# Opening of a hybrid decoder layer: two of four modulation sums computed by TensorE in one PSUM row, decay weights prepared later

## The chip, the cores and the metric

The kernel runs on one core of a Trainium2 chip. The metric is device time in microseconds (us) of one execution, lower is better. The kernel before takes 2497.76 us (median of 3 runs, 2494.24 to 2498.12).

The core has five engines with their own instruction streams: TensorE (PE, matrix products; its loads of the stationary operand are counted apart as PEld), VectorE (DVE), ScalarE (ACT), GpSimd (POOL) and SyncE (SP), which here issues nearly all DMA transfers. Each engine runs its instructions in a fixed order; a wait of one instruction holds up all that stand behind it on that engine.

## The reference

One layer, one sequence of 2048 tokens, model width 1024, all in float32. What matters here is the modulation and the decay:

```python
c_act = jax.nn.silu(c)                                   # (1, 1024)
mod = (c_act @ w_ada[l] + b_ada[l])[:, None, :]          # (1, 1, 6144)
sh_m, sc_m, g_m, sh_f, sc_f, g_f = jnp.split(mod, 6, axis=-1)
h = rmsnorm(x, pre_mix_norm_w[l]) * (1.0 + sc_m) + sh_m
proj = h @ w_in                                          # 3592 columns, 8 of them decay and beta logits a, b
g = -jnp.exp(dn_a_log) * jax.nn.softplus(a + dn_dt_bias)
```

After the projection come a gated DeltaNet with four heads, a short gated convolution, the output projection and a squared-ReLU MLP (1024 to 4096 to 1024) with the same norm and modulation. `h` of the first block of tokens can't be had before `sc_m` and `sh_m` are known, which need the first 2048 columns of `w_ada` (8 MB).

## The kernel before, in words

Tokens are worked on in four blocks of 512. `hT` (tiles `h`) is the normed and modulated block, transposed: eight tiles, one for each 128 of the 1024 model columns. Exact products are made from split operands: each float32 weight and each `h` is cast to a high part by ACT (L250, L275) and the remainder is subtracted by DVE or POOL (L251, L274 to L276), and three matmuls (L336) add high-high, high-low and low-high.

**The opening** is the first block. `c_act` comes from `c` at L123. Shift and scale of the mixer are made in four quarters; quarter `qd` covers two of the eight `h` tiles. For each quarter `ada_load` (L150) brings eight pieces of `w_ada`, 128 x 512 each (256 columns of scale, 256 of shift): the first and third into four `sb` slots, the second and fourth into two `w1h` tiles. `ada_first` multiplies each piece by a column of `c_act` and sums the eight (L160 and L162, DVE) to `wt`, which still has to be summed over its 128 partitions. `ada_affine` does that with four narrow matmuls with a column of ones (L172), and four ACT operations (L177, L179) add bias and norm weight and leave the columns `mod_m`. Then come two projection weights for some quarters (`load_w1`: a transfer to `w1s`, L250, L251), the transposes of x (L265), the modulation and split of two `h` tiles (L272 or L274, L275, L276), and the projection of what there is so far (L336, into up to four PSUM accumulators). So work on `h` starts before the whole modulation is there.

**The decay weights** are the eight columns of `w_in` for the logits. Their split into `wab` (L382, L383) stands ahead of `pre_norm_first`. `neg_a` is made in `gating` (L487 to L490), which runs after the opening: 16 matmuls (L446, L448) and a DVE copy (L451) begin a chain of small DVE operations; the convolutions (L433 to L440) and the first transposes and products per head (L543 to L578) follow. L544 writes `bco`, which the products at L578 wait for.

**The gates** of the mixer and the MLP come from `ada_acc` (L129 to L133): eight pieces of 128 x 1024 per gate through three `w2h` buffers, multiplied and summed on DVE beside the opening's end and the first heads.

The order of instructions on each engine is laid out by a scheduler when the program is built. It works on the operations in program order and puts them where it expects their operands; `tc.issue_after(x)` holds back what is written in its block until `x`. The pools decide how many buffers of a name there are: `tp` and `pd` in PSUM two each, `acc` four, `w1h`, `w1s` and `w2h` three each. The head of the loop that calls the functions of the opening:

```python
for qd in range(4):
    acc = ada_first(quarters[qd])
    if 1 <= qd < 3:
        quarters.append(ada_load(qd + 1))
    mod[qd] = ada_affine(*acc, 84 + 2 * qd, 60 + 2 * qd, 76 + 2 * qd, f"m{qd}")
```

Of the kernel before, what the change touches and what calls it, by code (L numbers as in the profile page):

```python
# [13 lines left out]
ALU = mybir.AluOpType  # L14
# [18 lines left out]
def hybrid_layer(  # L33
# [40 lines left out]
    def ps_d():  # L74
        return psum.tile([P, 2, 256], F32, name="pd", bufs=2)
# [76 lines left out]
                                  .rearrange("(k p) f -> p k f", p=P))  # L152
        return sts

    def ada_first(sts):
        acc = small.tile([P, 2, 256], F32, name="wt", bufs=2).rearrange("p j i -> p (j i)")
        for k in range(KT):
            sj = sts[k // 2][:, (k % 2) * TB:(k % 2 + 1) * TB]
            if k == 0:
                V.tensor_scalar(out=acc, in0=sj, scalar1=c_act[:, 0:1], scalar2=None, op0=ALU.mult)  # L160
            else:
                V.scalar_tensor_tensor(out=acc, in0=sj, scalar=c_act[:, k:k + 1], in1=acc,  # L162
                                       op0=ALU.mult, op1=ALU.add)
        return [acc[:, 256:512], acc[:, 0:256]]

    def ada_affine(acc_sc, acc_sh, c_sc, c_w, c_sh, tag):

        ps = ps_tp()
        w = acc_sc.shape[-1] // P
        for n, acc in enumerate((acc_sc, acc_sh)):  # L170
            for j in range(w):
                T.matmul(out=ps[:, n * w + j:n * w + j + 1], lhsT=acc[:, j * P:(j + 1) * P],  # L172
                         rhs=ones[:, 0:1], start=True, stop=True)
        mod = const.tile([P, 2, w], F32, name="mod_" + tag)
        sc, sh = mod[:, 0], mod[:, 1]
        for j in range(w):
            A.activation(out=sc[:, j:j + 1], in_=ps[:, j:j + 1], func=AF.Identity,  # L177
                         scale=cols[:, c_w + j:c_w + j + 1], bias=cols[:, c_sc + j:c_sc + j + 1])
            A.activation(out=sh[:, j:j + 1], in_=ps[:, w + j:w + j + 1], func=AF.Identity,  # L179
                         bias=cols[:, c_sh + j:c_sh + j + 1])  # L180
        return sc, sh
# [197 lines left out]

    quarters.append(ada_load(1))  # L380
    wab = const.tile([P, KT, 16], F32R, name="wab")
    V.tensor_copy(out=wab[:, :, 0:8], in_=wab_s)  # L382
    V.tensor_tensor(out=wab[:, :, 8:16], in0=wab_s, in1=wab[:, :, 0:8], op=ALU.subtract)  # L383

    r0 = const.tile([P, 2, NT], F32, name="r0")
    for t in range(NT):
# [23 lines left out]
    def pre_norm_first(hT):  # L410

        mod, ws, pss = [None] * 4, [], []
        for qd in range(4):
            acc = ada_first(quarters[qd])
            if 1 <= qd < 3:
                quarters.append(ada_load(qd + 1))
            mod[qd] = ada_affine(*acc, 84 + 2 * qd, 60 + 2 * qd, 76 + 2 * qd, f"m{qd}")
            for f0 in EARLY[qd]:
                ws.append(load_w1(w_in, f0 * P, V, True, hold=False))
                pss.append(ps_acc())  # L420
            for half in range(2):
                to_hT(hT, xn0[2 * half:2 * half + 2], half, mod, range(2 * qd, 2 * qd + 2, 2),
                      A if qd < 3 else V)
            for i, w in enumerate(ws):
                new = i >= len(ws) - len(EARLY[qd])
                proj(pss[i], w, hT, ks=range(0 if new else 2 * qd, 2 * qd + 2))
# [15 lines left out]
    def gating(hT):  # L442
# [41 lines left out]
        V.tensor_scalar(out=xa, in0=xa, scalar1=0.0, scalar2=None, op0=ALU.max)  # L484
        g = small.tile(s3, F32, name="gg", bufs=1)
        V.scalar_tensor_tensor(out=g, in0=p, scalar=2.0, in1=xa, op0=ALU.mult, op1=ALU.add)
        if not ada.get("neg_a"):  # L487
            A.activation(out=neg_a, in_=alog, func=AF.Exp)
            V.tensor_scalar(out=neg_a, in0=neg_a, scalar1=-1.0, scalar2=None, op0=ALU.mult)
            ada["neg_a"] = True  # L490
        V.tensor_tensor(out=g, in0=g, in1=bc(neg_a[:, None, :], s3), op=ALU.mult)
        gh = small.tile([P, 2, NT, NH], F32R, name="ghl", bufs=1)
        V.tensor_copy(out=gh[:, 0], in_=g)
# [671 lines left out]
```

## Time and profile before

| what | value |
|---|---|
| median of 3 runs | 2497.76 us |
| the profiled execution | 2501.52 us |
| its span in the trace | 2499.8 us |
| PE busy | 2416.5 us, 97% |
| PEld busy | 2011.4 us, 80% |
| DVE busy | 1764.7 us, 71% |
| ACT busy | 1170.9 us, 47% |
| POOL busy | 237.0 us, 9% |

The shares are averages over the span. Rows below give times from the span's start. "PEclk" is the clock of TensorE that was granted, 1.00 being 2.4 GHz and 0.50 being 1.2 GHz. A row in brackets ends with the idle time of the engine just before it and what ended that. Where several instructions of a line follow each other, a row holds them all, with their count behind the x. The time of one is better read from the distance of starts, since matmuls overlap.

### The profile page before, as it was taken

The page shows a single profiled execution, that of the slowest core. Times are in us where ns is not written, and L with a number is a line of the kernel's source. Part 1 is how long each engine was busy: PE and PEld are TensorE (multiplying, and loading weights), DVE is VectorE, ACT ScalarE, POOL GpSimd, SP SyncE. Part 2 cuts the span into 40 slices and gives each one's busy share as a digit, 9 for nine tenths or more (in the row PEclk, how much of TensorE's full clock was granted, in tenths as well). Part 3 has the DMA queues.
Part 4 walks back from the last instruction along what each step waited for, and adds up shares of the span by engine and source line. Part 5 has one row for each costly group of instructions (what it writes and reads, how often), then busy time and mean ns, then how long its engine had stood idle before and what let it go on. Part 6 is the DMA issues. An engine that isn't in the chain of part 4 may idle for free.

```text
span 2499.8 us, 33806 instructions
## 1 busy us (share of the span) xinstructions
PE 2416.5 (97%) x11874; PEld 2011.4 (80%) x11874; DVE 1764.7 (71%) x3833; ACT 1170.9 (47%) x2402; POOL 237.0 (9%) x391
## 2 busy tenths in 40 slices
PE   5889999999999999999999999999999999999998
PEld 3678887788778888888878888888887888888887
DVE  6777795877885568576697657756679556857675
ACT  5533552444563245544466145544456424654432
POOL 2513010000040201000012020000002120100000
PEclk9999999999999999999999999999999999999999
DMA  7788489855664542544475544345557454344453
GB/s 246 266 292 267 168 292 310 283 177 169 202 234 156 172 153 103 156 147 127 136 245 193 184 154 143 102 135 152 160 164 249 143 169 168 110 144 135 125 161 101
DMA packets 297268, 449.53 MB, mean 180 GB/s; under 512 B 39189, under 2 KB 195978, under 8 KB 282250
## 3 DMA queue, kind: packets, MB, share of 16 engines
q1 hardware_dynamic: 295584, 447.27, 54.5%
q8 instruction: 94, 1.54, 0.3%
q14 instruction: 76, 0.62, 0.1%
q10 hardware_dynamic: 1514, 0.09, 0.0%
HBM read 376.01 MB, written 71.30 MB: 179 GB/s over the span
## 4 chain that ended last, share of the span: by engine, by line
PE 75%; DVE 13%; DMA 7%; ACT 3%; issue 2%; POOL 0%; SPq 0%; ACTq 0%; DVEq 0%
PE acc L336 41%; PE acc L341 24%; DVE t L438 2%; DMA w2h<-in_w_ff_dram 2%; DMA w2h<-in_w_ada_dram 1%; PE pd L704 1%; DMA w1s<-in_w_ff_dram 1%; PE pd L336 1%; DMA ws<-w2h 1%; DVE w1h L251 1%; DVE sb L935 1%; PE pd L560 1%; PE tp L265 1%; PE tp L692 1%; DVE sb L850 1%
## 5 line engine op out<-in xcount | busy, mean ns | idle before, releaser
L336 PE MATMUL acc<-h,w1h 128*128 128x512 f32 x5184 | 1219.6, 392 | 0.0
L336 PEld LDWEIGHTS acc<-h,w1h 128*128 128x128 f32 x5184 | 968.2, 188 | 196.0 <-ACT w1h L250 0.2
L341 PE MATMUL acc<-w1h,sa 128*128 128x512 f32 x2556 | 594.6, 392 | 7.9 <-ACT w1h L250 4.1
L341 PEld LDWEIGHTS acc<-w1h,sa 128*128 128x128 f32 x2556 | 478.3, 188 | 110.0 <-DVE w1h L251 7.0
L251 DVE TENSOR_TENSOR w1h<-w1s,w1h 128x1024 fp32r<-128x1024 f32 x333 | 406.5, 1221 | 152.8 <-ACT w1h L250 152.6
L250 ACT CAST w1h<-w1s 128x1024 fp32r<-128x1024 f32 (+1 forms) x343 | 359.6, 1048 | 289.2 <-PE acc L341 195.9
L959 DVE TENSOR_TENSOR t<-t 128x512 f32<-128x512 f32 (+1 forms) x148 | 91.3, 620 | 182.0 <-ACT t L958 179.2
L958 ACT ACTIVATE t<-acc 128x512 f32<-128x512 f32 (+1 forms) x132 | 73.7, 558 | 246.7 <-PE acc L336 246.3
L276 POOL TENSOR_TENSOR h<-t,h 128x256 fp32r<-128x256 f32 x70 | 59.6, 857 | 1251.9 <-ACT h L275 1246.6
L438 DVE SCALAR_TENSOR_TENSOR t<-cb,cols,t 128x512 f32<-128x512 f32 x144 | 119.1, 831 | 65.7 <-ACT t L436 63.9
L251 DVE TENSOR_TENSOR w2h<-sa,w2h 128x512 fp32r<-128x512 f32 x128 | 87.5, 687 | 35.7 <-ACT w2h L250 35.1
L336 PE MATMUL acc<-h,sa 128*128 128x256 f32 (+1 forms) x672 | 102.6, 308 | 4.0 <-POOL h L276 1.5
L250 ACT CAST w2h<-sa 128x512 fp32r<-128x512 f32 x128 | 78.5, 619 | 58.7 <-DVE w2h L251 33.2
L341 PE MATMUL acc<-w2h,sa 128*128 128x512 f32 x420 | 101.4, 393 | 0.0
L336 PEld LDWEIGHTS acc<-h,sa 128*128 128x128 f32 x672 | 90.2, 195 | 10.5 <-POOL h L276 3.8
L925 DVE TENSOR_TENSOR sb<-acc,sb 128x512 f32<-128x512 f32 x148 | 96.4, 681 | 2.0 <-PE acc L341 2.0
L341 PE MATMUL acc<-w2h,sb 128*128 128x512 f32 x384 | 95.2, 400 | 1.8 <-DVE sb L842 0.9
L341 PEld LDWEIGHTS acc<-w2h,sa 128*128 128x128 f32 x420 | 77.7, 188 | 15.5
L341 PEld LDWEIGHTS acc<-w2h,sb 128*128 128x128 f32 x384 | 72.3, 191 | 20.6 <-DVE sb L842 2.8
L250 ACT CAST sa<-t 128x256 fp32r<-128x256 f32 (+1 forms) x145 | 70.5, 487 | 27.2 <-DVE t L959 26.9
L251 DVE TENSOR_TENSOR sa<-t,sa 128x256 fp32r<-128x256 f32 (+2 forms) x145 | 75.3, 520 | 4.0 <-ACT sa L250 1.4
L234 ACT ACTIVATE jk_w<-sb 128x512 bf16<-128x512 f32 x64 | 40.3, 630 | 58.9 <-DVE sb L876 31.1
(285 smaller groups left out, 2748.4 us busy)
## 6 DMA issues: line engine op xcount, KB each, us to landing
w1s<-in_w_ff_dram SPq DMA_DIRECT2D x213, 512.0 KB, 3.9
w1h<-wc SPq DMA_DIRECT2D x86, 1024.0 KB, 4.9
w1s<-ws SPq DMA_DIRECT2D x112, 512.0 KB, 4.0
wc<-w1h SPq DMA_DIRECT2D x30, 1024.0 KB, 7.3
sa<-in_x_dram SPq DMA_DIRECT2D x32, 512.0 KB, 4.8
w1s<-in_w_in_dram SPq DMA_DIRECT2D x32, 512.0 KB, 5.4
w2h<-in_w_ada_dram SPq DMA_DIRECT2D x32, 512.0 KB, 5.3
sa<-in_w_out_dram SPq DMA_DIRECT2D x32, 512.0 KB, 3.8
```

Source lines behind the costliest of these rows:

```text
L234: A.activation(out=junk(DM, "w")[:, :src.shape[-1]], in_=src, func=AF.Square, scale=float(DM) ** -0.5, accum_out=s)
L250: A.copy(out=hi, in_=src)
L251: eng.tensor_tensor(out=lo, in0=src, in1=hi, op=ALU.subtract)
L265: T.transpose(out=tp[:, j * 256 + i * P:j * 256 + (i + 1) * P], in_=xn[i][:, (k0 + j) * P:(k0 + j + 1) * P], identity=ident)
L276: (G if j or eng is A else V).tensor_tensor(out=hT[k][:, 1, cs], in0=tmp, in1=hT[k][:, 0, cs], op=ALU.subtract)
L336: T.matmul(out=ps[:, c0:c1], lhsT=w[a][:, k, :], rhs=hT[k][:, b, c0:c1], start=(k == 0 and n == 0), stop=(k == KT - 1 and n == 2))
L341: T.matmul(out=ps, lhsT=lhs[a], rhs=rhs[b], start=(start and n == 0), stop=(stop and n == 2))
L438: V.scalar_tensor_tensor(out=tmp, in0=cb[:, w:w + TB], scalar=conv_w[:, w, ft:ft + 1], in1=tmp, op0=ALU.mult, op1=ALU.add)
L560: T.matmul(out=pk[:, t - tp0], lhsT=kq[h][:, 0, t * P:(t + 1) * P], rhs=kq[h][:, :, t * P:(t + 1) * P], start=True, stop=True)
L925: V.tensor_tensor(out=accs[key], in0=ps, in1=accs[key], op=ALU.add)
L958: A.activation(out=a[:, c0:c1], in_=ps[:, c0:c1], func=AF.Relu)
L959: V.tensor_tensor(out=a[:, c0:c1], in0=a[:, c0:c1], in1=a[:, c0:c1], op=ALU.mult)
```

## The change

`ada_first` gets a flag `on_pe`, set for quarters 1 and 3 (the second and the fourth). With it the sum over the eight pieces and over the 128 partitions is one accumulation of eight float32 matmuls: the stationary operand is a column of `c_act` (128 x 1), the moving one is the piece (128 x 512), and the result is one row of 512 in a `pd` buffer. ACT copies the row to the first partition of `wt`. `ada_affine` then turns the row into columns with matmuls whose contraction is one long (`ones[0:1, 0:1]`). Quarters 0 and 2 stay on DVE. `decay_weights` now holds the split of `wab` and the two operations on `neg_a`, and is written behind the third quarter's last DVE sum.

```diff
+    def ada_first(sts, on_pe):
         acc = small.tile([P, 2, 256], F32, name="wt", bufs=2).rearrange("p j i -> p (j i)")
+        if on_pe:
+            ps = ps_d().rearrange("p a b -> p (a b)")[0:1, :]
+            acc = acc[0:1, :]
         for k in range(KT):
             sj = sts[k // 2][:, (k % 2) * TB:(k % 2 + 1) * TB]
-            if k == 0:
+            if on_pe:
+                T.matmul(out=ps, lhsT=c_act[:, k:k + 1], rhs=sj, start=(k == 0), stop=(k == KT - 1))
+            elif k == 0:
                 V.tensor_scalar(out=acc, in0=sj, scalar1=c_act[:, 0:1], scalar2=None, op0=ALU.mult)
             else:
-                V.scalar_tensor_tensor(out=acc, in0=sj, scalar=c_act[:, k:k + 1], in1=acc,
-                                       op0=ALU.mult, op1=ALU.add)
+                ada["sum"] = V.scalar_tensor_tensor(out=acc, in0=sj, scalar=c_act[:, k:k + 1], in1=acc,
+                                                    op0=ALU.mult, op1=ALU.add)
+        if on_pe:
+            A.copy(out=acc, in_=ps)
...
-                         rhs=ones[:, 0:1], start=True, stop=True)
+                         rhs=ones[0:acc.shape[0], 0:1], start=True, stop=True)
...
-    V.tensor_copy(out=wab[:, :, 0:8], in_=wab_s)
-    V.tensor_tensor(out=wab[:, :, 8:16], in0=wab_s, in1=wab[:, :, 0:8], op=ALU.subtract)
+    def decay_weights():
+        V.tensor_copy(out=wab[:, :, 0:8], in_=wab_s)
+        V.tensor_tensor(out=wab[:, :, 8:16], in0=wab_s, in1=wab[:, :, 0:8], op=ALU.subtract)
+        A.activation(out=neg_a, in_=alog, func=AF.Exp)
+        V.tensor_scalar(out=neg_a, in0=neg_a, scalar1=-1.0, scalar2=None, op0=ALU.mult)
...
-            acc = ada_first(quarters[qd])
+            acc = ada_first(quarters[qd], qd % 2)
+            if qd == 2:
+                with tc.issue_after(ada["sum"].ins):
+                    decay_weights()
...
-        if not ada.get("neg_a"):
-            A.activation(out=neg_a, in_=alog, func=AF.Exp)
-            V.tensor_scalar(out=neg_a, in0=neg_a, scalar1=-1.0, scalar2=None, op0=ALU.mult)
-            ada["neg_a"] = True
```

The diff moves line numbers. In the changed kernel L165 is the new matmul, L172 the new ACT copy and L167/L169 the DVE sums (before L160/L162); L181 is before's L172, L274 its L265, L345 its L336, L283/L285 its L274/L276, L260 its L251, L393/L394 its L382/L383, L396 its L489, L462/L464 its L446/L448, L467, L473 and L475 its L451, L457 and L459, L454 its L438, L560 its L544.

On PE, around the second quarter's sum, the order before (`ones,wt` are the sums over partitions, `ident,sa` the transposes of x, `acc` the projection; numbers behind `h` tell tiles apart):

```order
L172 MATMUL tp<-ones,wt 128x1 x4
L265 MATMUL tp<-ident,sa 128x128 x8
L172 MATMUL tp<-ones,wt 128x1 x4
L265 MATMUL tp<-ident,sa 128x128 x3
L336 MATMUL acc<-h_201,sa 128x512
L265 MATMUL tp<-ident,sa 128x128
L336 MATMUL acc<-h_201,sa 128x512 x2
L336 MATMUL acc<-h_202,sa 128x512 x3
L265 MATMUL tp<-ident,sa 128x128 x4
```

and of the changed kernel:

```order
L181 MATMUL tp<-ones,wt 128x1 x4
L165 MATMUL pd<-w1h,c_act 1x512
L274 MATMUL tp<-ident,sa 128x128 x4
L165 MATMUL pd<-w1h,c_act 1x512 x3
L274 MATMUL tp<-ident,sa 128x128 x4
L165 MATMUL pd<-w1h,c_act 1x512 x3
L345 MATMUL acc<-h_199,sa 128x512 x3
L345 MATMUL acc<-h_200,sa 128x512 x3
L165 MATMUL pd<-w1h,c_act 1x512
L181 MATMUL tp<-ones,wt 128x1 x4
L274 MATMUL tp<-ident,sa 128x128 x8
```

The second quarter's eight matmuls lie between the transposes of the first, and the first six projection matmuls stand ahead of the last of them.

On PE, at the fourth quarter, the order before (between its sum over partitions and `gating` 60 L336 follow, of which the first are here):

```order
L336 MATMUL acc<-h_206,sa 128x512 x3
L172 MATMUL tp<-ones,wt 128x1 x4
L265 MATMUL tp<-ident,sa 128x128 x4
L336 MATMUL acc<-h_201,sa 128x512 x2
L265 MATMUL tp<-ident,sa 128x128 x4
```

and of the changed kernel (four more L165 of this quarter stand further up, between transposes and projection of the third; L462 and L464 are `gating`):

```order
L345 MATMUL acc<-h_203,sa 128x512 x3
L345 MATMUL acc<-h_204,sa 128x512 x3
L165 MATMUL pd<-w1h,c_act 1x512 x3
L181 MATMUL tp<-ones,wt 128x1 x4
L274 MATMUL tp<-ident,sa 128x128 x8
L462 MATMUL tp<-h_199,wab 16x512
L464 MATMUL tp<-h_199,wab 8x512
```

All of the projection work on the first six `h` tiles now lies ahead of the fourth quarter's sum, and only the last 24 projection matmuls (tiles 205 and 206, after the fifth L462) behind it.

On DVE, around the copy that begins `gating`, the order before:

```order
L251 TENSOR_TENSOR w1h<-w1s,w1h 128x1024
L276 TENSOR_TENSOR h_207<-t_503,h_207 128x256
L131 TENSOR_SCALAR gate_m<-w2h,c_act 128x1024
L451 COPY t_552<-tp 16x512
L457 COPY t_559<-tp 128x64
L459 TENSOR_TENSOR ab<-t_559 128x32
```

and of the changed kernel:

```order
L131 TENSOR_SCALAR gate_m<-w2h,c_act 128x1024
L283 TENSOR_SCALAR t_496<-tp,mod_m_486 128x256
L133 SCALAR_TENSOR_TENSOR gate_m<-w2h,c_act,gate_m 128x1024
L285 TENSOR_TENSOR h_205<-t_496,h_205 128x256
L283 TENSOR_SCALAR t_509<-tp,mod_m_486 128x256
L133 SCALAR_TENSOR_TENSOR gate_m<-w2h,c_act,gate_m 128x1024
L285 TENSOR_TENSOR h_205<-t_509,h_205 128x256
L133 SCALAR_TENSOR_TENSOR gate_m<-w2h,c_act,gate_m 128x1024 x2
L467 COPY t_558<-tp 16x512
L133 SCALAR_TENSOR_TENSOR gate_m<-w2h,c_act,gate_m 128x1024
L473 COPY t_565<-tp 128x64
L133 SCALAR_TENSOR_TENSOR gate_m<-w2h,c_act,gate_m 128x1024
```

Before, one operation of the mixer's gate stands ahead of that copy; now five do, and two more stand between it and the next steps of `gating`. On SP the loads of the gates' pieces follow suit: 13 of them stand ahead of the eleventh weight load to `w1s`, where 7 did. From some 290 us on the order is the same in both.

## Rows read from the trace of the kernel before

**Rows 1.** Stretches: us, busy time by engine, PE clock, DMA share, GB/s.

```profile
33.00:43.00 10.00, 8.12 (x23) 5.62 (x23) 9.75 (x10) 5.94 (x16) 5.88 (x6) 1.00 0.89 293
53.00:72.00 19.00, 18.95 (x89) 13.65 (x88) 5.72 (x7) 9.47 (x18) 8.05 (x6) 1.00 0.81 257
72.00:133.00 61.00, 47.03 (x220) 37.92 (x221) 55.21 (x97) 35.22 (x76) 33.05 (x26) 0.96 0.70 243
133.00:290.00 157.00, 155.09 (x861) 132.26 (x860) 121.86 (x286) 66.55 (x176) 28.28 (x53) 0.99 0.81 273
```

**Rows 2.** PE in order of time: start us, us, what [idle before, releaser].

```profile
23.03 1.87 PE L172 MATMUL tp<-ones,wt 128*128 128x1 f32 x8 [14.84 <-DVE wt L162]
39.61 3.31 PE L336 MATMUL acc<-h,sa 128*128 128x512 f32 x6 [1.46 <-ACT h L275]
44.86 0.65 PE L265 MATMUL tp<-ident,sa 128*128 128x128 f32 x4
49.65 0.96 PE L336 MATMUL acc<-h,sa 128*128 128x512 f32 x3 [1.33 <-POOL h L276]
...
132.43 1.09 PE L578 MATMUL tp<-ident,sa 128*128 128x128 f32 x4 [9.22 <-DVE bco L544]
```

**Rows 3.** The chain that ended last, 55 to 114 us: start us, us, what.

```profile
55.11 13.19 PE acc L336 x58
...
96.46 7.04 POOL w1h L251
...
105.04 8.12 DMA w2h<-in_w_ada_dram
```

**Rows 4.** DVE in order of time, opening.

```profile
14.40 0.20 DVE L382 CAST wab<-t 128x64 fp32r<-128x64 f32 x1 [12.05 <-DMA t<-in_w_in_dram]
...
23.69 5.47 DVE L162 SCALAR_TENSOR_TENSOR wt<-w1h,c_act,wt 128x512 f32<-128x512 f32 x7
...
34.19 7.86 DVE L162 SCALAR_TENSOR_TENSOR wt<-sb,c_act,wt 128x512 f32<-128x512 f32 x7
```

**Rows 5.** SP in order of time, and a DMA issue row (count, size, us to landing).

```profile
14.40 0.88 SPq L150 DMA_DIRECT2D sb<-in_w_ada_dram  x2
...
sb<-in_w_ada_dram SPq DMA_DIRECT2D x16, 256.0 KB, 6.4
```

**Rows 6.** One float32 product with 512 columns elsewhere in the kernel.

```profile
603.00 1.88 PE L192 MATMUL tp<-gate_f,ones 128*128 128x512 f32 x4
```

**Rows 7.** Line 446, matmuls of 16 stationary columns: least/median/most ns, first and last start.

```profile
L446 PE MATMUL tp<-h,wab x32: 388/396/402, 68.1 to 1891.8; 128*16 128x512 f32 x32
```

**Rows 8.** ACT in order of time.

```profile
39.76 1.05 ACT L250 CAST sa<-w1s 128x1024 fp32r<-128x1024 f32 x1
...
44.54 0.27 ACT L179 ACTIVATE mod_m<-tp,cols 128x1 f32<-128x1 f32 x1
...
99.95 0.58 ACT L433 COPY cb<-acc 128x512 f32<-128x512 f32 x1
```

**Rows 9.** DVE in order of time, from the start of gating to 133 us.

```profile
72.02 0.68 DVE L451 COPY t<-tp 16x512 f32<-16x512 f32 x1 [11.47 <-PE tp L448]
...
74.06 0.74 DVE L438 SCALAR_TENSOR_TENSOR t<-cb,cols,t 128x512 f32<-128x512 f32 x1
...
78.05 1.27 DVE L133 SCALAR_TENSOR_TENSOR gate_m<-w2h,c_act,gate_m 128x1024 f32<-128x1024 f32 x1
...
87.41 3.45 DVE L133 SCALAR_TENSOR_TENSOR gate_m<-w2h,c_act,gate_m 128x1024 f32<-128x1024 f32 x1
...
101.71 4.16 DVE L438 SCALAR_TENSOR_TENSOR t<-cb,cols,t 128x512 f32<-128x512 f32 x2 [0.45 <-ACT t L436]
...
113.19 1.28 DVE L133 SCALAR_TENSOR_TENSOR gate_m<-w2h,c_act,gate_m 128x1024 f32<-128x1024 f32 x1 [4.49 <-DMA w2h<-in_w_ada_dram]
...
118.08 2.91 DVE L438 SCALAR_TENSOR_TENSOR t<-cb,cols,t 128x512 f32<-128x512 f32 x1
...
127.60 2.86 DVE L438 SCALAR_TENSOR_TENSOR t<-cb,cols,t 128x512 f32<-128x512 f32 x1
```

More of the change, by code (lines that the diff above doesn't have):

```diff
@@ L153, in ada_load @@
         return sts
-    def ada_first(sts):
+    def ada_first(sts, on_pe):
         acc = small.tile([P, 2, 256], F32, name="wt", bufs=2).rearrange("p j i -> p (j i)")
+        if on_pe:
+            ps = ps_d().rearrange("p a b -> p (a b)")[0:1, :]
+            acc = acc[0:1, :]
         for k in range(KT):
             sj = sts[k // 2][:, (k % 2) * TB:(k % 2 + 1) * TB]
-            if k == 0:
+            if on_pe:
+                T.matmul(out=ps, lhsT=c_act[:, k:k + 1], rhs=sj, start=(k == 0), stop=(k == KT - 1))
+            elif k == 0:
                 V.tensor_scalar(out=acc, in0=sj, scalar1=c_act[:, 0:1], scalar2=None, op0=ALU.mult)
             else:
-                V.scalar_tensor_tensor(out=acc, in0=sj, scalar=c_act[:, k:k + 1], in1=acc,
-                                       op0=ALU.mult, op1=ALU.add)
+                ada["sum"] = V.scalar_tensor_tensor(out=acc, in0=sj, scalar=c_act[:, k:k + 1], in1=acc,
+                                                    op0=ALU.mult, op1=ALU.add)
+        if on_pe:
+            A.copy(out=acc, in_=ps)
         return [acc[:, 256:512], acc[:, 0:256]]
```

## The prediction, made before the changed kernel ran

> **What bounds the kernel now.** I read the busy shares first, then the opening by stretches, then PE's own order of time with the waits in it, then the chain that ended last, and last DVE and ACT where PE waits. PE is 97% busy over the whole span, so what matters is where it is not. From 133 to 290 us it works 155.09 of 157 [rows 1], and from about 290 us on both kernels have one order; a shift at 133 us is therefore carried to the end unchanged. What happens before has four stages.
>
> Up to 23 us PE waits: its first sum over partitions starts at 23.03 after 14.84 of idleness, released by DVE's first quarter [rows 2]. From 33 to 43 it is busy 8.12 of 10, and DVE, which sums the quarters, 9.75 [rows 1]. From there PE is bound by itself: the reader is to see one wait of 1.33, at 49.65, and between 53 and 72 it works 18.95 of 19 [rows 1, 2]. The chain names its work there: 58 projection matmuls in 13.19 [rows 3]. The third stage ends with the copy that begins gating, at 72.02, for which DVE had waited 11.47 [rows 9]. In the fourth, DVE is the bound: 55.21 of the 61 us to 133, and PE's wait of 9.22 before 132.43 is ended by DVE's `bco` [rows 1, 2]. So the question is what the change does to two dates: the copy at 72.02, and the release at 132.43.
>
> **What the change removes and adds.** DVE loses two sums of eight operations. PE gets 16 float32 matmuls of 512 columns; ACT two copies. The trace has no such matmul with one stationary column. Its nearest rows: the float32 products at 603.00 take 1.88 for two of them (each stands in the trace as two records), so 0.94 each [rows 6], against 13.19/58 = 0.23 for a projection matmul of as many columns [rows 3]. Fewer stationary columns don't help: of the matmuls of gating, with 16 and 8 columns, 16 stand between the first start, 68.1 [rows 7], and the copy at 72.02 [rows 9], 0.24 each, no less than a projection matmul. I take 0.94, with 0.23 as the lower end and 1.9 as the upper: PE ran at half rate in the early opening. Six projection matmuls at 39.61 take 3.31 [rows 2], and they would take 1.4 at 0.23; from 43 us on the distance of starts is 0.23.
>
> **Stage 1, to the first quarter's sum.** The decay weights' cast holds DVE until 14.40, waiting 12.05 for a transfer [rows 4]. With it moved behind the third quarter `c_act` can come some 4 us sooner. But two of the first quarter's pieces are issued only at 14.40 to 15.28 and land 6.4 later by the median [rows 5], near 21 to 22; the last two products have to follow. Before, the first quarter's sum ended at about 23.0. I take 1 us of gain (0 to 1.3).
>
> **Stage 2, second quarter.** Before, DVE's seven products behind the first take 5.47 from 23.69 [rows 4]. After, the eight matmuls stand between transposes, and PE has gaps there (10 - 8.12 = 1.9 in 33 to 43 [rows 1], more before). At 0.94 they are 7.5, at half rate 15. The sum would be in PSUM at 36 to 38, or at 43; then the copy (0.58 [rows 8]), eight small matmuls and four ACT operations make the second quarter's modulation ready near 40 (39 to 46), later than DVE made it. What follows is late by as much: the second weight's cast (39.76 [rows 8]) goes to about 42, and since its subtraction stands in DVE's order ahead of the last two products of the third quarter, the third sum ends near 45, where it ended at 42.05 (34.19 + 7.86 [rows 4]). The third modulation, ready at 44.8 before [rows 8], comes near 49.5. So far this costs little. At 49.65 before had 70 of its 96 projection matmuls still to do (the 58 of the chain's row, the three at 49.65 and nine between them); the changed order has 72 behind the third modulation.
>
> By the Trainium skill, "TensorE: Matmul & The Clock Gate", section "What's actually happening", the throttled clock is the default and activity releases it. That speaks for the change, which gives PE work where it had waited. If the full rate came at 30 rather than 43 us, some 12 projection matmuls would each save 0.2 and nine transposes 0.1, 3.5 in all, and the sum below would be lower by that. The windows before carry a granted clock of 1.00 throughout the opening [rows 1], while six matmuls took 3.31 [rows 2]: they don't show the level there, so I keep this out of the sum.
>
> **Stage 3, to the copy that begins gating.** The working for before: at 49.65, 70 projection matmuls of 0.23 (16.2), eight transposes of 0.16 (0.65/4 [rows 2]; 1.3), eight records of sums over partitions (half of the 1.87 at half rate [rows 2], 0.95), 16 gating matmuls (3.7) make 22.15, so 71.8 against the 72.02 seen. After, from the same 49.65: 72 x 0.23 = 16.6, seven of the fourth quarter's float32 matmuls at 0.94 = 6.6, 16 transposes 2.6, 0.95 and 3.7: 30.4, 8.3 more. The last quarter's chain adds the copy (0.58) and ACT's and DVE's modulation and split behind it, with only nine gating matmuls (2 us) as cover; before, 60 projection matmuls covered all of this. I add 1. The copy comes 9.5 later (5 if the fp32 matmuls fall into waits of PE or the clock comes sooner; 14 if the last quarter's chain lies open).
>
> **Stage 4, to the release of `bco`.** DVE goes on from the copy. By the order, 10 gate products and 30 convolution products stand before between the copy and the first L555 behind it; after, 11 and 27, so one more of 1.27 and three fewer of 0.74 [rows 9]: -0.95. DVE's wait of 4.49 at 113.19 was for a piece of the gate whose transfer took 8.12 behind a POOL split of 7.04 [rows 3, 9]. Its issue now stands ahead of the weight loads; it may go: 0 to -4.5. But 13 gate loads, where there were seven, stand ahead of the eleventh weight load on SP, and all of them share three buffers that DVE must free. Behind such a load a weight waits, behind the weight a head's projection, and behind that the convolution products: new waits of 0 to 4. Two gate products also stand between the steps of gating, 1.27 each. I take -4.5 for the wait, +2 for the new ones and -0.95: -3.5 (-5.4 to +3). PE's own clock and the seven projection matmuls that changed sides of the stall cancel to under 1.6, which I leave out.
>
> The sum: 9.5 - 3.5 = +6. DVE's 16 removed operations count for nothing here: their time was DVE's in stage 2, which PE's sum replaces by a later one. On the profiled execution that is 2501.52 + 6 = 2507.5. The median of the runs is 3.8 below that execution, so the time is 2497.76 + 6 = 2503.8. This case's own range is 2500 to 2509.
>
> **Rivals.**
>
> *The late gating is swallowed.* The chain from 96 to 113 goes through POOL's split, SP and the gate's transfer, not through gating [rows 3]. If these keep their dates, DVE's order after 113 does too, and a copy 9.5 late is made good out of the 9.22 that PE waits at 132.43 anyway. Against it: DVE is busy 55.21 of 61 there, without slack for a start 9.5 later. Time 2498 to 2500, taken as 2499.
>
> *The fourth stage shortens by more than the opening grows.* Four DVE operations in it are far above their usual length: 3.45 for 1.27, 4.16 for two of 0.74, 2.91 and 2.86 for 0.74 [rows 9], 9.2 in excess. If they find their places elsewhere, and the wait of 4.49 goes with no new one, the stretch from copy to release shrinks from 60.4 by 0.95 + 4.5 + 9.2 = 14.6 to 45.8, against 9.5 lost: -5.1, 2492.7. It decides when the stretch takes under 50.9. For it: POOL was busy 33.05 in those 61 us [rows 1], so the long ones depend on where POOL's work falls. Against it: the amount of POOL work is the same.
> The Trainium skill, "SBUF — State Buffer", section "SBUF: two separate sides", says that a DVE operation with two SBUF inputs and a POOL operation lock each other out of a shared port pair. The rows agree: the seven products took 7.86 beside POOL's work and 5.47 where it had little [rows 4]. By that rule the excess would move rather than go.
>
> *PE stays at half rate.* If the second quarter's eight matmuls run at 1.9 each and the modulation is ready only at 46, the third comes some 5 later: +11, 2509. For it: the earlier stretch of PE did not leave half rate until 43. Against it: the new matmuls fill gaps.
>
> That the change does not do what it says I rule out; the order shows it.
>
> **Chances.** The forecast 0.50, the swallowed start 0.25, the shorter fourth stage 0.15, half rate 0.10. A measurement of this kernel can tell about 0.2%, 5.0 us, from no change: 2492.8 and 2502.8 are the bounds. Of the forecast's own range some four fifths lie above 2502.8 (0.39), and all of half rate (0.10): slower 0.49. Of the shorter stage most lies beyond 2492.8 (0.13): faster 0.13. The rest is same: 0.38. For 8 in 10 the range goes from 2493, where the shorter stage begins to be left out, to 2512, three above half rate for a chain of the last quarter that lies open.
>
> **What would show it.** In the profile after: starts of the new matmuls (L165) 0.94 apart (0.23 would take 11 us of the cost away); the third modulation at 49.5 and the fourth near 71 (49.65 + 48 x 0.23 + 6.6 + 1.3 + copy, sums and ACT 2); the gating copy (L467) at 81.5; PE busy near full from 50 to there; DVE's wait for a gate piece gone or replaced by a wait behind weights; the stall before the products per head (L590) ending at 138.4. The forecast is wrong if the copy comes before 77, or if from copy to release takes less than 51 or as much as 60.

## The result and the profile after

The changed kernel takes 2520.32 us (median of 4 runs, 2519.33 to 2523.12), the kernel before 2497.94 in the runs beside it: ratio 1.0087, 95% interval 1.0075 to 1.01. That is 22.4 us slower, where 6 had been predicted and 14 was the far end of the range. The direction was right and the loss in the opening lay where it was predicted; some 9 us more arose behind the release of `bco`, in a stretch that had been taken as fixed.

The profiled execution after took 2523.12 us, with a span of 2521.4 against 2499.8. PE is busy 2439.8 us where it was 2416.5, DVE 1760.5 where it was 1764.7: the 16 operations taken from DVE barely show, while the 16 products given to PE hold it for 17.6 of the 23.3 us more. The stretches that answer to [rows 1] (us, busy time and count of PE, PEld, DVE, ACT, POOL, then PE clock, DMA share, GB/s), with the two stretches of half clock that matter below:

```profile
33.00:43.00 10.00, 7.14 (x29) 2.95 (x27) 5.90 (x7) 5.45 (x14) 3.28 (x5) 0.90 0.87 287
53.00:72.00 19.00, 17.00 (x72) 10.81 (x71) 5.44 (x5) 6.82 (x15) 7.93 (x5) 0.99 0.81 276
72.00:143.00 71.00, 58.60 (x255) 45.18 (x253) 62.30 (x103) 38.70 (x84) 30.42 (x29) 0.91 0.73 247
143.00:300.00 157.00, 153.05 (x839) 129.39 (x838) 118.04 (x278) 63.20 (x160) 31.46 (x54) 0.99 0.76 253
140.10:146.90 6.80, 4.80 (x17) 4.09 (x17) 4.43 (x17) 4.14 (x15) 0.52 (x2) 0.50 0.74 252
300.50:310.70 10.20, 8.88 (x29) 7.72 (x30) 2.54 (x5) 4.19 (x17) 0.00 (x0) 0.50 0.00 0
```

The fourth row is the one to compare with the last of [rows 1]. Before, the 157 us behind the release of `bco` held 2 us of idle PE; after, as many hold 4, and right behind them the granted clock falls to half for 10.2 us. Before, the corresponding fall lasts 3.4 us:

```profile
288.90:292.30 3.40, 3.40 (x10) 2.63 (x9) 0.69 (x1) 2.31 (x10) 0.00 (x0) 0.50 0.00 0
```

PE's own order of time after (start us, us, what [idle before, releaser]), the rows that answer to [rows 2]:

```profile
20.66 1.87 PE L181 MATMUL tp<-ones,wt 128*128 128x1 f32 x8 [12.53 <-DVE wt L169]
22.45 1.87 PE L165 MATMUL pd<-w1h,c_act 128*1 128x512 f32 x2
...
29.88 2.73 PE L165 MATMUL pd<-w1h,c_act 128*1 128x512 f32 x6
...
40.41 0.73 PE L345 MATMUL acc<-h,sa 128*128 128x512 f32 x2 [1.80 <-ACT sa L259]
...
47.37 0.95 PE L181 MATMUL tp<-ones,wt 128*128 128x1 f32 x8
...
64.99 2.74 PE L165 MATMUL pd<-w1h,c_act 128*1 128x512 f32 x6
68.39 1.05 PE L181 MATMUL tp<-ones,wt 1*128 1x1 f32 x8 [0.66 <-ACT wt L172]
...
107.60 0.58 PE L512 MATMUL tp<-gg,tri 128*128 128x16 f32 x2 [4.71 <-DVE gg L503]
...
142.10 1.09 PE L590 MATMUL tp<-ident,sa 128*128 128x128 f32 x4 [5.61 <-DVE bco L556]
```

Each product stands as two records. At full rate three take 2.74, 0.91 each (0.94 was taken from [rows 6]); the first one, at 22.45, took 1.87 at half rate. The stall before the products per head shrank from 9.22 to 5.61, but it ends at 142.10 instead of 132.43.

DVE after, around gating (as [rows 9]) and at the release:

```profile
79.99 2.61 DVE L133 SCALAR_TENSOR_TENSOR gate_m<-w2h,c_act,gate_m 128x1024 f32<-128x1024 f32 x2 [4.35 <-DMA w2h<-in_w_ada_dram]
82.66 0.68 DVE L467 COPY t<-tp 16x512 f32<-16x512 f32 x1
83.78 1.28 DVE L133 SCALAR_TENSOR_TENSOR gate_m<-w2h,c_act,gate_m 128x1024 f32<-128x1024 f32 x1 [0.45 <-DMA w2h<-in_w_ada_dram]
...
141.88 0.15 DVE L556 TENSOR_TENSOR bco<-bco,grec 128x8 f32<-128x8 f32 x1
```

The copy that begins gating comes at 82.66, where 81.5 had been written down; the wait for a gate's piece has moved ahead of it (4.35) instead of behind it.

Where the rest of the loss arises is seen at the mixer's end. After:

```profile
294.55 1.02 PE L201 MATMUL tp<-gate_m,ones 128*128 128x512 f32 x2
...
296.89 1.13 PE L201 MATMUL tp<-gate_m,ones 128*128 128x512 f32 x2 [0.86 <-DVE sb L793]
298.09 1.05 PE L181 MATMUL tp<-ones,gate_f 128*128 128x1 f32 x8
299.01 1.03 PE L181 MATMUL tp<-ones,sb 128*128 128x1 f32 x8
301.82 1.87 PE L181 MATMUL tp<-ones,gate_f 128*128 128x1 f32 x8 [1.78 <-ACT mod_f L188]
303.55 1.84 PE L181 MATMUL tp<-ones,sb 128*128 128x1 f32 x8
305.25 8.71 PE L350 MATMUL acc<-w2h,sb 128*128 128x512 f32 x26
...
324.68 0.84 PE L350 MATMUL acc<-w2h,sb 128*128 128x512 f32 x3
```

and before:

```profile
281.77 1.98 PE L192 MATMUL tp<-gate_m,ones 128*128 128x512 f32 x4 [0.87 <-DVE sb L781]
...
287.58 1.03 PE L172 MATMUL tp<-ones,sb 128*128 128x1 f32 x8
288.47 6.41 PE L341 MATMUL acc<-w2h,sb 128*128 128x512 f32 x20
...
305.61 0.84 PE L341 MATMUL acc<-w2h,sb 128*128 128x512 f32 x3
```

The mixer's gate is summed over partitions by two float32 products on PE (L192 before, L201 after; called the gate sums here). They stood together before; after, they stand 2.3 us apart, the second pair of sums waits 1.78 for ACT, and what follows runs at half rate until 310.7: 26 output products in 8.71 us. The row of three output products that closes each list is the last mark used below: 19.1 us later after than before. From there on PE, DVE, ACT and POOL have the same order in both; at the end of the two traces the lag is 21.6.

### The profile page after: what moved, and what is told of

It reads as the page before. It is cut to its first block, busy times and chain, and to the rows that moved or that the text cites. A ratio compares the mean times of both kernels' runs of the same rounds, so it can differ in the third digit from the quotient of the medians.

```text
span 2521.4 us, 33871 instructions
## 1 busy us (share of the span) xinstructions
PE 2439.8 (97%) x11906; PEld 2015.9 (80%) x11906; DVE 1760.5 (70%) x3817; ACT 1172.4 (46%) x2404; POOL 230.6 (9%) x391
## 4 chain that ended last, share of the span: by engine, by line
PE 75%; DVE 13%; DMA 6%; ACT 4%; issue 2%; ACTq 0%; SPq 0%; POOL 0%; DVEq 0%
PE acc L345 41%; PE acc L350 25%; DVE t L454 2%; PE pd L716 1%; DVE w1h L260 1%; DMA w2h<-in_w_ff_dram 1%; DMA w1s<-in_w_ff_dram 1%; DMA w2h<-in_w_ada_dram 1%; PE pd L572 1%; DVE sb L947 1%; PE pd L345 1%; DMA ws<-w2h 1%; PE tp L704 1%; DVE sa L521 1%; PE tp L692 1%
## 5 line engine op out<-in xcount | busy, mean ns | idle before, releaser
L345 PE MATMUL acc<-h,w1h 128*128 128x512 f32 x5184 | 1223.2, 393 | 0.0
L345 PEld LDWEIGHTS acc<-h,w1h 128*128 128x128 f32 x5184 | 969.1, 188 | 196.2 <-ACT w1h L259 0.2
L260 DVE TENSOR_TENSOR w1h<-w1s,w1h 128x1024 fp32r<-128x1024 f32 x333 | 407.0, 1222 | 155.5 <-ACT w1h L259 155.4
L285 POOL TENSOR_TENSOR h<-t,h 128x256 fp32r<-128x256 f32 x70 | 59.6, 854 | 1258.1 <-ACT h L284 1252.3
L454 DVE SCALAR_TENSOR_TENSOR t<-cb,cols,t 128x512 f32<-128x512 f32 x144 | 117.2, 822 | 69.0 <-ACT t L452 67.2
L260 DVE TENSOR_TENSOR w2h<-sa,w2h 128x512 fp32r<-128x512 f32 x128 | 87.6, 688 | 40.1 <-ACT w2h L259 39.7
L345 PE MATMUL acc<-h,sa 128*128 128x256 f32 (+1 forms) x672 | 100.8, 307 | 2.9 <-ACT sa L259 1.8
L345 PEld LDWEIGHTS acc<-h,sa 128*128 128x128 f32 x672 | 90.8, 196 | 12.2 <-ACT h L284 3.6
L260 DVE TENSOR_TENSOR sa<-t,sa 128x256 fp32r<-128x256 f32 (+2 forms) x145 | 75.5, 521 | 3.9 <-ACT sa L259 1.4
L284 ACT CAST h<-t 128x256 fp32r<-128x256 f32 x128 | 49.1, 407 | 40.4 <-DVE t L283 39.3
```

What stands on the lines that cost most here:

```text
L260: eng.tensor_tensor(out=lo, in0=src, in1=hi, op=ALU.subtract)
L284: A.copy(out=hT[k][:, 0, cs], in_=tmp)
L285: (G if j or eng is A else V).tensor_tensor(out=hT[k][:, 1, cs], in0=tmp, in1=hT[k][:, 0, cs], op=ALU.subtract)
L345: T.matmul(out=ps[:, c0:c1], lhsT=w[a][:, k, :], rhs=hT[k][:, b, c0:c1], start=(k == 0 and n == 0), stop=(k == KT - 1 and n == 2))
L454: V.scalar_tensor_tensor(out=tmp, in0=cb[:, w:w + TB], scalar=conv_w[:, w, ft:ft + 1], in1=tmp, op0=ALU.mult, op1=ALU.add)
```

## The experiments

Three marks are read in every trace: the gating copy (72.02 before), the start of the DVE operation that completes `bco` (132.20), and the row of three output products (305.61, called the mixer's mark). The table gives how much later each comes than before, in us, and the difference of medians against the runs of before beside it. The marks are read in one execution of each kernel. All kernels but "both quarters, decay as before" hold the move of the decay weights.

| kernel | copy | bco | mixer's mark | time, us | ratio (95%) |
|---|---|---|---|---|---|
| the change | +10.6 | +9.7 | +19.1 | +22.4 | 1.0087 (1.0075 to 1.01) |
| decay weights only | -0.9 | -0.7 | 0.0 | -2.5 | 0.9992 (0.9982 to 1.0002) |
| + second quarter | +8.7 | +5.7 | +7.0 | +5.9 | 1.0025 (1.0016 to 1.0033) |
| + fourth quarter | +10.1 | +9.5 | +15.0 | +14.6 | 1.0058 (1.0044 to 1.0072) |
| both quarters, decay as before | +15.3 | +14.7 | +24.1 | +24.9 | 1.0099 (1.0084 to 1.0113) |
| half of the products | +10.1 | +6.6 | +11.8 | +12.2 | 1.0047 (1.0031 to 1.0062) |
| products that nobody reads | +8.8 | +6.8 | +9.1 | +9.7 | 1.0036 (1.0024 to 1.0048) |
| MLP's sums in the other pool | +14.1 | +13.3 | +23.1 | +24.9 | 1.0097 (1.0084 to 1.011) |
| gates late | -1.5 | -9.5 | +17.1 | +19.2 | 1.0072 (1.0059 to 1.0084) |
| gate of the mixer early | 0.0 | -6.0 | +5.1 | +5.5 | 1.0023 (1.0013 to 1.0034) |
| gate sums in the other pool | +13.9 | +13.1 | +16.8 | +16.1 | 1.0065 (1.0053 to 1.0078) |
| the same on decay weights only | -1.5 | -1.6 | -1.0 | -0.1 | 0.9998 (0.9989 to 1.0007) |

The last mark tells the time to within 3.5 us in all of them; `bco` does not.

**Decay weights only**

```diff
-            acc = ada_first(quarters[qd], qd % 2)
+            acc = ada_first(quarters[qd], False)
```

> All four quarters summed on VectorE as before; only the decay weights and neg_a stand behind the third quarter. Theory A (the whole loss comes from float32 products put on TensorE where it is the bound): the first quarter's sum ends 1 to 2.5 us sooner and nothing is lost; 2495 to 2499 us, against 2497.9 before. Rival B (half of the loss is a new layout behind the opening, which any shift of the opening brings): 2501 to 2510.

2496.97 us against 2499.46, an interval that just holds no change. Theory A stands. The first quarter's sum over partitions starts at 21.84 instead of 23.03.

**The second quarter alone on TensorE** (the flag is `qd == 1`)

> Decay weights behind the third quarter as in the changed kernel; the second quarter alone is summed by TensorE. Theory A: its eight products fill TensorE's gaps up to 40 us, and the opening's bound stretch gets only a late third quarter: gating copy at 74 to 78 us instead of 72.0, time 2498 to 2504. Rival B: the opening shifts little, the layout changes all the same: 2505 to 2512. Rival C (TensorE's earlier work raises the clock at 27 instead of 43 us and VectorE is free for the fourth quarter): below 2496.

2505.32 us against 2499.46: 5.9 more, past the end of A's range as a time, just inside it as a difference (2504 - 2497.9 = 6.1). A's mark was missed: the gating copy came at 80.77, not at 74 to 78. The products were not hidden in PE's gaps, and PE in that stretch still has waits of 0.66, 1.80, 1.49 and 1.18. That the later second modulation causes them, by pushing the casts and splits behind it, is read from the order and was not tested. Rival B's time was met but not its condition, since the opening shifted by 8.7. C is out: the granted clock did rise early, at 30.5, but fell to half again for 6.8 us from 40.7 and for 6.8 from 54.4. Up to `bco` 3.0 of the 8.7 are made good.

**The fourth quarter alone** (`qd == 3`)

> Decay weights behind the third quarter; the fourth quarter alone is summed by TensorE. Theory A: 7 or 8 products of 0.94 us and the open chain of the last quarter fall into the stretch in which TensorE never waits, so the gating copy comes 7 to 10 us later than 72.0 and the time is 2510 to 2520, most of the loss of 22.4. Rival B: about the same as the second quarter alone.

2514.08 against 2499.46: 14.6, within A's range. But the copy and `bco` are late by no more than 10.1 and 9.5; another 5.5 arise up to the mixer's mark, where the gate sums stand apart as in the changed kernel:

```profile
292.94 1.13 PE L201 MATMUL tp<-gate_m,ones 128*128 128x512 f32 x2 [0.86 <-DVE sb L793]
...
297.86 1.87 PE L181 MATMUL tp<-ones,gate_f 128*128 128x1 f32 x8 [1.78 <-ACT mod_f L188]
```

The same two waits, 0.86 and 1.78, as after. Rival B is out (14.6 against 5.9), but A's price and open chain are not the whole either: more than a third of the loss is made far behind the opening, where the layout differs.

**Both quarters, decay weights as before**

```diff
+    decay_weights()
...
-            if qd == 2:
-                with tc.issue_after(ada["sum"].ins):
-                    decay_weights()
```

(`neg_a` went back into gating.)

> Second and fourth quarter summed by TensorE as in the changed kernel, decay weights and neg_a where the kernel before had them. Theory A: the move of the decay weights neither costs nor saves more than 2 us: 2518 to 2523. Rival D (the move is part of the loss, since its operations now stand between the third sum and the weights): 2505 to 2515.

2524.35 against 2499.46, 24.9 slower: past A's range as a time, inside it as a difference (20.1 to 25.1). The move is no part of the loss. The runs with the second and with the fourth quarter alone both hold its -2.5, which is not clear of noise; counted once, the two make 5.9 + 14.6 + 2.5 = 23.0, where the change costs 22.4. So the two prices about add up.

**Half of the products**

```diff
-                T.matmul(out=ps, lhsT=c_act[:, k:k + 1], rhs=sj, start=(k == 0), stop=(k == KT - 1))
+                if k < 4:
+                    T.matmul(out=ps, lhsT=c_act[:, k:k + 1], rhs=sj, start=(k == 0), stop=(k == 3))
```

> The changed kernel with four instead of eight products in each of the two quarters on TensorE; the other half of these two sums is left out. If the price of the float32 products is the cost (0.91 us each in the trace): eight fewer, the gating copy 5 to 7.4 us sooner than 82.7, and 2505 to 2514 us. Rival (the handing over costs: the copy of the row, the sum over one partition, the last quarter's open chain, whatever the number of products): copy at 80 to 83 and 2517 to 2521.

The time is 2510.47 against 2498.25, 12.2 more where the whole change costs 22.4. The copy missed what was expected: 82.16, where the change has 82.66 (86.17 and 85.91 in two more executions of its opening, below). PE's clock accounts for much of that. With fewer products PE had waits of 1.41 and 2.12 early on, and a long stretch at half rate:

```profile
37.10:50.80 13.70, 11.57 (x34) 7.41 (x34) 3.55 (x7) 7.61 (x21) 4.14 (x6) 0.50 0.51 158
```

In the change only 3.4 us of that stretch were at half rate (41.1 to 44.5, by the clock of 0.90 in its window). 10 us more at half rate are 5 us of work not done, most of the 7.3 that eight products less give. In the two other executions of the change's opening 6.8 us were at half rate, so that the size of this is open. So the number of products counts, but this run did not measure it cleanly, and it also has the gate sums together at the mixer's end.

**Products that nobody reads** (decay weights only, and for the fourth quarter, behind its transposes)

```diff
+            if qd == 3:
+                ps = ps_d().rearrange("p a b -> p (a b)")[0:1, :]
+                for k in range(KT):
+                    T.matmul(out=ps, lhsT=c_act[:, k:k + 1],
+                             rhs=quarters[3][k // 2][:, (k % 2) * TB:(k % 2 + 1) * TB],
+                             start=(k == 0), stop=(k == KT - 1))
```

> All quarters summed on VectorE, decay weights behind the third (2497.0 us); in addition TensorE computes the fourth quarter's eight float32 products into a row that nobody reads, behind that quarter's transposes. Price alone, without its chain: the gating copy 7.4 us later than 71.1, at 78 to 79, and 2500 to 2505 us. Rival (the loss of the fourth quarter is its open chain and the layout behind it): copy below 74, 2496 to 2499.

2507.94 against 2498.25. Here nothing waits for the products, and the kernel is 9.7 us slower than before all the same (12.2 against the decay weights only, which stood at -2.5), above the 2505 that I gave as the end for the price. Ten of the sixteen records stand in one row:

```profile
65.17 4.45 PE L443 MATMUL pd<-w1h,c_act 128*1 128x512 f32 x10
...
72.31 4.84 PE L345 MATMUL acc<-h,sa 128*128 128x512 f32 x20 [1.29 <-POOL h L285]
```

Five products in 4.45, 0.89 each; a wait for POOL of 1.29 that the kernel without them does not have; and a half-rate stretch from 38.3 of 10.2 us instead of 6.8. 8 x 0.9 + 1.3 + 1.7 = 10.2, near the 9.8 by which the copy is later than with the decay weights only (80.87 against 71.11). So the products, with the wait and the low clock that came with them but no chain, cost at the copy nearly what the fourth quarter costs there (10.1 later than before, 11.0 than with the decay weights only): the open chain of the last quarter adds little more than 1.

**The MLP's sums in the other pool**

```diff
-        ps = ps_tp()
+        ps = ps_d().rearrange("p a b -> p (a b)") if tag[0] == "f" else ps_tp()
```

> The changed kernel; the MLP's four sums over partitions use the other PSUM pool, so that the second pair need not wait for ScalarE to have read the first (1.78 us at 301.8, followed by half clock until 310.7). If that wait and the low clock behind it are 5.4 us of the loss: 2514 to 2518. Rival (they only show a lag that is elsewhere): 2519 to 2523.

2523.17 against 2498.25, no better than the change. The wait of 1.78 is gone, but the gate sums still stand apart, a new wait of 2.47 came in at 310.2, and the clock was at half for 6.8 us from 294.0 and 3.4 from 311.1. This edit missed; the layout there is settled by another edit, the last but one.

**Gates late** (decay weights only; the gates' products held behind the first `bde`)

```diff
-                jobs.pop(0)()
+                with tc.issue_after(ada["bde"].ins):
+                    jobs.pop(0)()
```

> All quarters on VectorE, decay weights behind the third (2497.0 us); the gates' products are held behind the first pair's bde on VectorE, which takes some ten of them (12 us) out of the stretch from gating to bco, in which VectorE is the bound. If that stretch is bound by VectorE's work: the stall of 7.7 before L590 goes or shrinks, 2488 to 2493. Rival (the work comes back behind it, where the first heads' products need VectorE): 2496 to 2505.

The stretch from copy to `bco` was bound by DVE as thought: it shrank from 60.4 with the decay weights only to 52.1, `bco` came at 122.69, the stall before the heads' products fell from 7.70 to 1.89. And the kernel became 19.2 us slower. PE's waits from 120 to 300 us (what waits <- for what: us in total, times, longest):

```profile
PE acc L345 <- ACT w1h L259: 7.3, 3, 3.3
PE acc L345 <- DVE w1h L260: 6.2, 3, 4.5
```

Projection waits for its weights, 13.5 us in all, which it does in that stretch neither before nor after. On SP six gate loads take from 163.65 to 177.29, waiting for buffers that DVE must free, and weight loads stand behind them. Besides, the granted clock was at half for 17.1 us between 188 and 237. The gain of 9.5 was given back almost three times over. That the work comes back behind `bco`, as the rival has it, is so, but the loss is past the rival's range and shows at the projection's weights, not at the first heads' products.

**The mixer's gate early** (as the one before, but that gate is written at the end of the opening)

> All quarters on VectorE, decay weights behind the third. The mixer's gate is written at the end of the opening, so that its eight products (10 us) stand on VectorE ahead of the gating copy, where it idled 11 us; the MLP's gate products stay held behind the first bde. If the stretch from copy to bco is bound by VectorE's work and the earlier loss of the late gates came from too many products behind bco: bco 7 to 9 us sooner than 131.5, and 2488 to 2493 us. Rival (SyncE's queue decides: gate loads that wait for a buffer hold up the weight loads behind them, early as well as late): 2498 to 2510.

2504.94 against 2499.46. `bco` is 6.0 sooner than before (5.3 than with the decay weights only, where 7 to 9 was expected), and 11.1 are lost behind it. Of these the trace shows waits of PE of 3.83 (for POOL, at 236.8), 1.86 and 1.07, and 248 projection products ahead of the release instead of 263, 15 x 0.23 = 3.4. Again a gain at `bco` did not reach the end; whether SP's queue is the cause, as the rival has it, was not isolated.

**The gate sums in the other pool** (the changed kernel, with its order of PE unchanged up to the output projection)

```diff
-            ps = ps_tp()
+            ps = ps_d().rearrange("p a b -> p (a b)")
             T.matmul(out=ps, lhsT=ones, rhs=gt[:, hs], start=True, stop=True)
```

> The changed kernel; the two float32 gate products at the mixer's end use the other PSUM pool. TensorE's order is that of the changed kernel up to there. If the way the gate products stand apart, with waits of 0.86 and 1.78 and half clock until 310.7 behind them, is part of the loss: the first 30 products of the output projection (21.2 us in the changed kernel, 15.7 before) take 15 to 17, and the time is 2514 to 2517. Rival (the lag of 14 us that exists ahead of it decides and the rest evens out): 2519 to 2523.

2515.59 against 2499.46: 16.1 of the 22.4 are left. The mixer's end now reads:

```profile
291.12 1.88 PE L201 MATMUL pd<-gate_m,ones 128*128 128x512 f32 x4
...
302.90 1.03 PE L181 MATMUL tp<-ones,sb 128*128 128x1 f32 x8
303.92 7.78 PE L350 MATMUL acc<-w2h,sb 128*128 128x512 f32 x26
...
322.42 0.84 PE L350 MATMUL acc<-w2h,sb 128*128 128x512 f32 x3
```

No waits; half clock for 3.4 us instead of 10.2. From `bco` to the mixer's mark it is 177.1 us, where the change takes 182.8 and before takes 173.4. So 5.7 of the loss are made there, by the way the gate sums lie and not by the quarters' products. The execution with the MLP's sums moved had nearly the same opening as this one (`bco` at 145.53 and 145.35), with the gate sums apart: there it is 183.2 us.

**The same edit on the decay weights only**

> All quarters on VectorE, decay weights behind the third, gate products in the other PSUM pool. If that frees TensorE's wait of 0.9 at 282 and no more: 2495 to 2497 us. Rival (another order there, as bad as in the changed kernel): 2500 to 2504.

2499.39 against 2499.46, between the two ranges. Where the gate sums had stood together the edit gives nothing. None of these kernels beats the kernel before clearly; the decay weights alone come nearest.

## Why the prediction was right, and where it failed

**Right.** *The price of a product.* 0.94 was taken from another kind of float32 product; 0.91 is measured (0.89 where ten records stand in a row). One stationary column is no cheaper.

*The dates of the opening.* ACT ends the third modulation at 49.3 (49.5 predicted) and the fourth at 70.4 (71); the copy comes at 82.66 (81.5). The first date is partly luck: DVE's third sum ended at 43.5, not near 45, but PE came to it only at 47.37, behind 16 projection products, the first of them at half rate (until 44.5). PE was not near full up to the copy either, as I had it: the last quarter's chain left waits of 0.66, 0.40 and 0.58, for which I had added 1, and 3.4 us at half rate from 71.8, some 1.7 of work, were in no term of the sum. The changed opening was met in three profiles, with copies at 82.7, 86.2 and 85.9: it varies by 3.5 between executions, with the first quarter's sum (20.66, 21.79, 22.21) and with a half-rate stretch of 3.4 or 6.8 us near 41. That is 10.6, 14.1 and 13.9 later than before: of my 9.5, with bounds 5 and 14, two executions reach the upper bound. The rival of half rate is out: the second modulation was ready at 37.9, not at 46.

*That DVE's relief counts for nothing.* DVE idles 9.02 at 30.09 for ACT's cast after its sums are gone.

*The clock.* By the trace's record the granted clock rises at 27.4, amid PE's first products, where before it rose only at 43.1. PE was busy 9.69 us of the 10 from 23 to 33, where it was 6.02 before. In the six profiles with the second quarter on PE the clock rises between 27.4 and 32.7, in the seven others between 34.1 and 47.2. By the Trainium skill, "TensorE: Matmul & The Clock Gate", section "What's actually happening", activity releases the throttle; the trace agrees (1.87 for the product at 22.45, 0.91 each from 29.88 on). The 3.5 us that I kept out of the sum do not show at the third modulation (49.3, where 49.5 was worked out without them); the clock had fallen again at 41.1, and how the rest divides was not settled.

**Too small.** *Stage 4*, from copy to `bco`: I took -3.5, the stretch measures 59.2 instead of 60.2, so -1.0. The wait of 4.49 behind the copy did go, but DVE found others: 0.45 for a gate's piece and 3.39 for ACT before 119.09. With the copy's 10.6 that makes +9.7 at `bco`, where I had +6.0. The runs with the second quarter alone and with half of the products gain 3.0 and 3.5 there, near my -3.5; those with the whole fourth quarter on PE gain 0.6 to 1.0. The rival of a swallowed start is out: in every run with products most of the shift reaches `bco`. So is the shorter fourth stage, which needed less than 50.9; the long DVE operations went elsewhere (3.46 at 99.48 for 1.27, 2.35 at 104.36 and 2.31 at 138.15 for 0.17).

**Wrong: the step "a shift at 133 us is therefore carried to the end unchanged".** It rested on one order of both kernels from about 290 us on and on PE being busy 155 of 157 in between. The lag went from 9.7 at `bco` to 19.1 at the mixer's mark, in two parts:

- Up to 287.65, where the output projection begins (273.38 before): +14.3, 4.6 more. In the traces 256 projection products start ahead of the release after and 263 before: seven, 7 x 0.23 = 1.6. I had seen them and let them cancel against PE's clock; the half clock behind the restart was longer instead: 146.9 - 142.1 = 4.8 us against 135.3 - 132.4 = 2.9, so 0.95 of work. Waits of 1.06, 0.36 and 1.44 against 0.20 and 0.56 make 2.1. Sum 4.65.
- From there to the mark: 19.1 - 14.3 = 4.8. The wait of 1.78, and 6.8 us more at half rate, so 3.4: 5.2.

The rows of the first part, after:

```profile
156.46 0.66 PE L590 MATMUL tp<-ident,sa 128*128 128x128 f32 x4 [1.06 <-ACT sa L456]
...
162.20 0.66 PE L565 MATMUL tp<-ident,t 128*128 128x128 f32 x4 [0.36 <-ACT t L456]
...
247.35 0.71 PE L704 MATMUL tp<-sa,w2t 128*128 128x128 f32 x4 [1.44 <-ACT w2t L698]
...
287.65 1.52 PE L350 MATMUL acc<-w2h,sb 128*128 128x512 f32 x6
```

and before, with its half clock at the restart as a stretch (as [rows 1]):

```profile
155.42 1.10 PE L560 MATMUL pd<-sa 128*128 128x256 f32 x4 [0.20 <-DVE sa L568]
...
231.22 0.71 PE L692 MATMUL tp<-sa,w2t 128*128 128x128 f32 x4 [0.56 <-ACT w2t L686]
...
273.38 1.52 PE L341 MATMUL acc<-w2h,sb 128*128 128x512 f32 x6
128.50:135.30 6.80, 2.87 (x11) 2.62 (x12) 6.32 (x19) 1.26 (x3) 1.80 (x3) 0.50 0.58 181
```

The first part is worked out from the traces; no run takes it away by itself. But it comes again in two other runs with both quarters on PE: 4.3 with the decay weights as before and 4.5 with half of the products, with 256 and 255 projection products ahead of the release. (In the two runs with a changed pool other work begins the mixer's end, so that this mark is not the same.) With one quarter alone it is 1.2 (the second) and 0.9 (the fourth), with 261 ahead. The second part is shown by the run that moved two products to another pool: 5.7 back between `bco` and the mark, 6.3 in the difference of medians. It comes again, as 4.7 and 5.1, in the two other runs with the wait of 1.78, and is under 0.8 with the decay weights only, with the second quarter, with half of the products and with those that nobody reads. It belongs to the fourth quarter: the second quarter alone keeps the gate sums together and carries its lag on as I had assumed (+5.7, +7.0, +5.9), and the fourth alone does not (+9.5, +15.0, +14.6). Why the scheduler sets them apart there was not found. Of the last 3.3 us, between +19.1 at the mark and +22.4 in the medians, 2.5 lie behind the mark in the two traces (21.6 at their end) and were not followed; executions of one kernel differ by as much (2494.24 to 2498.84 before), and the profile after met the shortest of the three openings.

The chances were built on the same step: the range ended where a carried lag ends. Of the 22.4 some 10 stand at `bco`, where +6 was predicted, and some 9 come from stretches that I had taken as fixed. Of the 16.4 by which +6 was too small the copy makes 1.1 (the parts of its sum give 9.3, entered as 9.5), stage 4 makes 2.5, the lag that was to stay unchanged 9.4, and what is left 3.3. Neither of my two signs of being wrong came, a copy before 77 or 60 us from copy to release: both lay ahead of the place where most of the error arose.

## What to carry to other kernels

A float32 product on the engine that bounds the stretch costs its full length, 0.91 us here with a result of one row: eight products that nobody read made the kernel 9.7 us slower than before. Work taken from an engine that is not the bound need gain nothing. Where a scheduler lays out the program, an edit in the opening has to be followed through the order of every engine for as long as the orders differ, here 300 us, and each place where a wait or a half clock can arise is a term of the sum. A date in the middle of such a stretch is not a result: `bco` 9.5 us sooner went with a kernel 19 us slower.

## What the runs showed of the hardware

Less work on PE can go with less clock: with half of the products the granted clock fell back to 0.50 for 13.7 us from 37.1 (one profile), with all of them for 3.4, 6.8 and 6.8 us from some 41 in three executions that had the same order and nearly the same waits. What decides between 3.4 and 6.8 is not shown.

A short wait can go with a longer stretch at half rate. At the mixer's end, behind rows of matmuls with one moving column, the clock falls in nearly every profile: for 3.4 us in the seven with the gate sums together and no wait between the MLP's sums, for 10.2 to 10.3 us in the three with the wait of 1.78 between those. In the changed kernel 26 output products took 8.71 us behind that wait, where 26 without it took 7.78 (303.92, other pool), part of it still at half rate.

A float32 product with one stationary column and 512 moving ones took 0.91 us at full rate and 1.87 at half, no less than the 0.94 of one with 128 stationary columns [rows 6].
